# Six of 31 convolution taps per channel block as ScalarE products summed by accumulating transfers, and scans over their own input

## The chip, the cores and the metric

The kernel runs on one core of one Trainium2 chip. A core has a matrix engine (TensorE, PE in the profile; its weight loads are shown as PEld), a vector engine (VectorE, DVE), an activation engine (ScalarE, ACT), a general engine (GpSimd, POOL) and an engine that issues transfers here (SyncE, SP). Every engine takes its own instructions strictly in the order in which they were compiled, and waits on semaphores for the others. The metric is the device time of one execution in microseconds (us). A lower time is better.

## The reference

The reference is one layer of a diffusion backbone: 512 latent tokens of width 1024 with a prefix of 256 context tokens, in float32. Around the part that is changed stand two gated feed-forward blocks. The changed part is the mixer, with two branches over one input projection:

```
def conformer_branch(u_glu, lp):
    v, gt = jnp.split(u_glu, 2, axis=-1)
    u = v * jax.nn.sigmoid(gt)
    u = depthwise_conv(u, lp["w_dw"], lp["b_dw"], (15, 15))      # 31 taps, 1024 channels
    u = jax.nn.silu(layernorm(u, lp["g_ln"], lp["b_ln"]))
    return u @ lp["w_conf_out"]

def rglru_direction(xr, ...):                    # 1280 channels, forward and backward in time
    r  = sigmoid(einsum(xb, w_a) + b_a)          # blocks of 128 channels
    ig = sigmoid(einsum(xb, w_x) + b_x)
    log_a = -LRU_C * r * softplus(-lam)
    a  = exp(log_a)
    bb = sqrt(-expm1(2.0 * log_a)) * (ig * xr)
    return linear_scan(a, bb, h0, reverse)       # h[t] = a[t] * h[t-1] + bb[t]

y_lru = ((hf + hb) * gelu(proj_gate)) @ lp["w_lru_out"]
y = (sig(g_conf) * y_conf + sig(g_lru) * y_lru) @ lp["w_out"]
```

## The kernel before

Channels lie on the 128 partitions and tokens along the free dimension, so a block of 128 channels over the 512 latent tokens is one tile of 128x512, and with the context 128x768. There are eight blocks in the conformer branch and ten in the recurrent one.

Products on PE need float32 accuracy and are made from split operands. `wsplit` (L168 to 171) takes a weight tile that SP loaded (`wload`, L155 to 163, four buffers), has ACT write its rounded high half (`whi`, L152) and DVE the remainder (`wlo`, L153), three buffers each. PE then makes three products: high by high (L179), high weights by the low half of the data (L181), low weights by the high half (L183). So a weight tile goes through SP, ACT, DVE and PE in that order, and this pipeline runs through the whole kernel. The splits are issued at high priority.

The mixer is written as a list of steps (`ORDER`, L35 to 38), which a scheduler then turns into one instruction order per engine by priorities and by dependences. The steps are: `c` projects one conformer block and multiplies it by its sigmoid (`conv_block`), and `conv_taps` follows it; `f` projects one recurrent block, makes its four-tap convolution and splits it (`lru_front`); `w` loads and splits the gate weights of one block; `a` and `s` make the two gates of each direction (`lru_gates`) and then the exponent, the square root and the two scans (`lru_scan`); `g` makes two output gates (`lru_gate`); `o` multiplies the sum of the scans by its gate (`lru_out`).

`conv_taps` (L850 to 864) is the depthwise convolution of one block: ACT writes the first tap with the bias (L862), and DVE adds the other 30, each as one multiply and add over 128x512 (L864), with the result in place in `cv`. It has a priority lower by 5000 than all else, so the scheduler puts these taps into the room between other instructions. Block 7 makes five taps on PE instead and comes after the mixer, as `LATE` says.

In `lru_scan` ACT writes the decay `a` (L907), a tanh (L910) and a square root over the gate `r`; DVE multiplies into `r` (L915), then into the gated input `ig` (L916), and scans into `h`, which is `r` (L919 to 923). The sum of the two directions is written into `r` of the first one (L926). These tiles come from rotating buffers whose numbers stand in `BUFS`: three of `r`, `ig` and `a`, one pair `wgh`, `wgl` of split gate weights. When a new block takes a buffer, its first write waits until the last reader of the block before is done.

Behind the mixer stand, in this order, the merge gates of the recurrent branch (`lat_gate`, `merge_gate`, `dense`), the split of the mixer's output `y` (L153), the recurrent output projection with the gated sum (L1024), the merge gates of the conformer branch with the layer norm over all eight `cv` (L1026 to 1038) in their midst, and the conformer output projection. All of these are products on PE with new weights.

## Time and profile before

| | us |
|---|---|
| median of 3 runs | 1471.4 (1469.43 to 1475.37) |
| profiled execution, its own time | 1472.69 |
| its span in the profile | 1470.9 |
| PE busy in the span | 1423.0 (97%) |
| DVE busy | 1223.8 (83%) |
| ACT busy | 714.4 (49%) |
| POOL busy | 12.4 (1%) |

The profile is of one execution. Its span is 1.8 us shorter than the execution's own time. Busy time of PE is the time in which it had work in its pipeline. The shares are means over the whole span. The mixer fills the stretch from about 580 to 875 us, and the projections behind it start there. POOL clears the edges of two kinds of tile (`ux`, `u`) in the mixer and does little else; all transfers of the kernel before are issued by SP.

### The profile page before, as it was taken

To read this page: it belongs to the slowest core of one execution; us is meant where nothing else is said; L and a number is where in the kernel's file an instruction comes from. 1 tells how busy PE (TensorE), PEld (TensorE's weight loads), DVE (VectorE), ACT (ScalarE), POOL (GpSimd) and SP (SyncE) were. 2 spreads that over 40 slices of the span, in tenths; PEclk is the share of its full clock that TensorE was granted. 3 is DMA by queue.
4 is the path that set the end of the run, shared out by engine and by line. 5 is a ranking of instruction groups with operands and counts; after the bars stand their busy time and mean duration, and the time that the engine had idled before them with its cause. 6 is when DMAs were issued, how large, how long until landed. Compare 5 with 4: busy or idle time off the path is not lost.

```text
span 1470.9 us, 20684 instructions
## 1 busy us (share of the span) xinstructions
PE 1423.0 (97%) x8166; PEld 1283.6 (87%) x8166; DVE 1223.8 (83%) x1868; ACT 714.4 (49%) x992; POOL 12.4 (1%) x55
## 2 busy tenths in 40 slices
PE   6999999999999998999999989999999999999997
PEld 5998999989998987787788778778899989999896
DVE  6899997777878768999999999976677869678686
ACT  4632432414322446678878862236365525345253
POOL 0000000000000000000000020000000000000000
PEclk9999999999999999999999999999999999999999
DMA  9335352343543234222222223233341333323331
GB/s 375 116 129 180 115 172 72 130 143 101 186 137 137 85 100 148 82 66 78 79 73 79 72 64 93 86 116 143 103 152 49 99 103 98 112 94 99 102 100 58
DMA packets 48627, 166.41 MB, mean 113 GB/s; under 512 B 5520, under 2 KB 7824, under 8 KB 47888
## 3 DMA queue, kind: packets, MB, share of 16 engines
q1 hardware_dynamic: 48528, 165.08, 33.9%
q8 instruction: 64, 1.05, 0.3%
q14 instruction: 35, 0.29, 0.1%
HBM read 160.86 MB, written 4.19 MB: 112 GB/s over the span
## 4 chain that ended last, share of the span: by engine, by line
PE 43%; DVE 14%; issue 2%; ACT 1%; DMA 1%; DVEq 0%; ACTq 0%
PE psm L183 9%; PE psm L179 9%; PE psm L181 9%; PE psm L452 4%; PE psm L454 4%; PE psm L453 4%; DVE cv L864 3%; DVE wlo L153 2%; PE ps L179 1%; PE ps L181 1%; PE ps L183 1%; DVE ig L916 1%; DVE r L915 1%; DVE ig L900 1%; DVE r L923 1%
## 5 line engine op out<-in xcount | busy, mean ns | idle before, releaser
L152 ACT ACTIVATE whi<-raw 128x1024 fp32r<-128x1024 f32 (+2 forms) x218 | 220.3, 1012 | 333.0 <-PE psm L181 231.3
L153 DVE TENSOR_TENSOR wlo<-raw,whi 128x1024 fp32r<-128x1024 f32 (+2 forms) x218 | 252.5, 1159 | 25.7 <-ACT whi L152 25.3
L864 DVE SCALAR_TENSOR_TENSOR cv<-u,vec,cv 128x512 f32<-128x512 f32 x236 | 165.0, 741 | 0.6 <-ACT cv L862 0.3
L179 PE MATMUL psm<-H,whi 128*128 128x256 f32 (+1 forms) x496 | 151.9, 355 | 2.6 <-ACT H L152 1.7
L183 PE MATMUL psm<-H,wlo 128*128 128x256 f32 (+1 forms) x496 | 151.6, 353 | 0.3 <-DVE wlo L153 0.2
L181 PE MATMUL psm<-H,whi 128*128 128x256 f32 (+1 forms) x496 | 151.5, 353 | 0.0
L179 PE MATMUL psm<-nh,whi 128*128 128x512 f32 (+2 forms) x376 | 141.2, 383 | 4.6 <-ACT u L846 2.9
L183 PE MATMUL psm<-nh,wlo 128*128 128x512 f32 (+2 forms) x376 | 140.6, 379 | 2.4 <-DVE wlo L153 2.4
L181 PE MATMUL psm<-nl,whi 128*128 128x512 f32 (+2 forms) x366 | 138.6, 385 | 1.7 <-DVE nl L332 1.5
L179 PEld LDWEIGHTS psm<-H,whi 128*128 128x128 f32 x496 | 93.0, 189 | 16.2 <-ACT H L152 2.2
L183 PEld LDWEIGHTS psm<-H,wlo 128*128 128x128 f32 x496 | 93.6, 189 | 14.0 <-DVE wlo L153 1.3
L181 PEld LDWEIGHTS psm<-H,whi 128*128 128x128 f32 x496 | 93.9, 189 | 13.2 <-issue 0.2
L452 PE MATMUL psm<-nbx,whi 128*128 128x384 f32 x266 | 89.6, 337 | 1.3 <-ACT whi L152 0.5
L454 PE MATMUL psm<-nbx,wlo 128*128 128x384 f32 x266 | 89.4, 336 | 0.3 <-DVE wlo L153 0.3
L179 PEld LDWEIGHTS psm<-nh,whi 128*128 128x128 f32 x376 | 70.4, 189 | 18.5 <-ACT u L846 3.2
L183 PEld LDWEIGHTS psm<-nh,wlo 128*128 128x128 f32 x376 | 70.6, 189 | 16.0 <-DVE wlo L153 3.3
L181 PEld LDWEIGHTS psm<-nl,whi 128*128 128x128 f32 x366 | 68.9, 189 | 16.2 <-DVE nl L332 3.0
L642 DVE SCALAR_TENSOR_TENSOR x<-psm,m,x 128x512 f32<-128x512 f32 x64 | 47.8, 746 | 39.6 <-PE psm L183 39.6
L247 DVE SCALAR_TENSOR_TENSOR raw<-raw,cb 128x1024 f32<-128x1024 f32 x56 | 68.2, 1219 | 14.0 <-DMA raw<-in_wmod 13.8
L453 PE MATMUL psm<-nbx,whi 128*128 128x384 f32 x228 | 76.6, 336 | 0.0
L152 ACT ACTIVATE whi<-s 128x1024 fp32r<-128x1024 f32 x38 | 40.3, 1062 | 72.7 <-PE psm L181 40.0
L452 PE MATMUL psm<-nb,whi 128*128 128x256 f32 x228 | 65.8, 288 | 0.8 <-DVE t L493 0.8
(379 smaller groups left out, 3759.6 us busy)
## 6 DMA issues: line engine op xcount, KB each, us to landing
raw<-in_up SPq DMA_DIRECT2D x88, 512.0 KB, 3.7
raw<-in_wmod SPq DMA_DIRECT2D x56, 512.0 KB, 3.3
raw<-in_down SPq DMA_DIRECT2D x30, 512.0 KB, 3.9
raw<-in_down SPq DMA_DIRECT2D x24, 384.0 KB, 3.2
mod<-in_wmod SPq DMA_DIRECT2D x16, 512.0 KB, 11.1
raw<-in_wvg SPq DMA_DIRECT2D x16, 512.0 KB, 3.7
raw<-in_wout SPq DMA_DIRECT2D x11, 512.0 KB, 3.8
raw<-in_wlx SPq DMA_DIRECT2D x10, 512.0 KB, 3.7
```

What stands on the lines that cost most here:

```text
L152: S.activation(hi, src, AF.Copy)
L153: V.tensor_tensor(lo, src, f32(hi), op=ALU.subtract)
L179: T.matmul(p_, hi[:, wk, :], h, start=first, stop=False)
L181: T.matmul(p_, hi[:, wk, :], l, start=False, stop=False)
L183: T.matmul(p_, lo[:, wk, :], h, start=False, stop=last)
L247: V.scalar_tensor_tensor(o, raw, 1.0, cb[j], op0=ALU.mult, op1=ALU.mult, accum_out=out[:, j:j + 1])
L452: T.matmul(ps, hi[:, o + k, :], h, start=first and k == 0, stop=False, **kw)
L453: T.matmul(ps, hi[:, o + k, :], l, start=False, stop=False, **kw)
L454: T.matmul(ps, lo[:, o + k, :], h, start=False, stop=k == 3, **kw)
L642: V.scalar_tensor_tensor(x[:, d], ps[-1], g[:, d, 0:1], x[:, d], op0=ALU.mult, op1=ALU.add)
L864: V.scalar_tensor_tensor(o, u[:, t:t + SEQ], wdw[:, j, t:t + 1], o, op0=ALU.mult, op1=ALU.add)
L900: V.scalar_tensor_tensor(ig, ig, 1.0, xr, op0=ALU.add, op1=ALU.mult)
```

## The change

For the conformer blocks 0 to 6 the last six of the 31 taps are not made by DVE. ACT makes each as a product of the shifted input with its weight. The first one is written into a tile `o2`; the other five are written into a tile `tp`, and POOL issues a transfer for each that adds `tp` to `o2` on its way. When all are in, DVE adds `o2` to the result. `o2` and `tp` have one buffer each. The scans write over their own input `ig` instead of `r`, their sum goes straight into the tile `y`, and the output gate is multiplied in place. The gate weights get a second pair of buffers. The list of steps is the same. In the changed kernel, lines from 45 on are one number higher, and those behind `conv_taps` ten; the product is L871, the transfer L873 and the addition L874.

```diff
@@ -40,8 +40,9 @@
 UB, TC_, TA, T2 = 4, 8, 4, 8
 NPE = 8
 NB = 2
-BUFS = {"ux": 2, "acc": 1, "xr": 3, "xh": 2, "xl": 2, "r": 3, "ig": 3, "a": 3, "ge": 2, "wgh": 1, "wgl": 1}
+BUFS = {"ux": 2, "acc": 1, "xr": 3, "xh": 2, "xl": 2, "r": 3, "ig": 3, "a": 3, "ge": 2, "wgh": 2, "wgl": 2}
 PET = {7: 5}
+NDMA = {j: 6 for j in range(7)}
 SK = 3
 DGB = 3
 PAT = {6: 0, 7: 3}
@@ -860,8 +861,17 @@
         with tc.high_priority(offset=-LOW):
             if not n_pe:
                 S.activation(o, u[:, :SEQ], AF.Identity, scale=wdw[:, j, 0:1], bias=b_dw[:, j:j + 1])
-            for t in range(max(1, n_pe), TAPS):
+            n_dma = NDMA.get(j, 0)
+            for t in range(max(1, n_pe), TAPS - n_dma):
                 V.scalar_tensor_tensor(o, u[:, t:t + SEQ], wdw[:, j, t:t + 1], o, op0=ALU.mult, op1=ALU.add)
+            if n_dma:
+                o2 = Y.tile([P, SEQ], F32, name="o2", tag="o2", bufs=1)
+                for t in range(TAPS - n_dma, TAPS):
+                    tp = o2 if t == TAPS - n_dma else Y.tile([P, SEQ], F32, name="tp", tag="tp", bufs=1)
+                    S.activation(tp, u[:, t:t + SEQ], AF.Copy, scale=wdw[:, j, t:t + 1])
+                    if tp is not o2:
+                        GP.dma_start(o2, tp, accum_op=ALU.add)
+                V.tensor_tensor(o, o, o2, op=ALU.add)
 
     def lru_front(b):
         wt = wsplit(wload(io["wlx"][b // 2][:, b % 2 * 1024:b % 2 * 1024 + 1024], 1024), 0, 1024, KB)
@@ -914,7 +924,7 @@
                 last["sqrt"] = S.activation(r, r, AF.Sqrt, scale=0.25, bias=tiny)
             V.scalar_tensor_tensor(r, a, 1.0, r, op0=ALU.add, op1=ALU.mult)
             V.tensor_tensor(ig, ig, r, op=ALU.mult)
-            h = r
+            h = ig
             if d == 0:
                 V.tensor_tensor_scan(h, a, ig, 0.0, op0=ALU.mult, op1=ALU.add)
             else:
@@ -922,9 +932,8 @@
                                      op0=ALU.mult, op1=ALU.add)
                 V.tensor_tensor_scan(h[:, CTX:][:, ::-1], a[:, CTX:][:, ::-1], ig[:, CTX:][:, ::-1], h[:, 0:1],
                                      op0=ALU.mult, op1=ALU.add)
-        hsum = R[0][:, CTX:]
-        V.tensor_tensor(hsum, R[0][:, CTX:], R[1][:, CTX:], op=ALU.add)
-        return hsum
+        y[b] = blocks(Y, "y", LB + 1, F32)[0]
+        V.tensor_tensor(y[b], I[0][:, CTX:], I[1][:, CTX:], op=ALU.add)
 
     def lru_gate(i):
         raw = wload(io["wlg"][i], 2048)
@@ -942,12 +951,11 @@
             ge.append(g)
         return ge
 
-    def lru_out(b, g, hsum):
-        y[b] = blocks(Y, "y", LB + 1, F32)[0]
-        V.tensor_tensor(y[b], g, hsum, op=ALU.mult)
+    def lru_out(b, g):
+        V.tensor_tensor(y[b], y[b], g, op=ALU.mult)
 
     us = {}
-    fronts, gates, hsums, wgs, scans = {}, {}, {}, {}, {}
+    fronts, gates, wgs, scans = {}, {}, {}, {}
     for step in ORDER.split():
         kind, n = step[0], int(step[1:])
         if kind == "c":
@@ -963,13 +971,13 @@
             gs = scans.pop(n, [])
             for d in range(len(gs), 2):
                 gs.append(lru_gates(n, d, wgs[n], fronts[n]))
-            hsums[n] = lru_scan(n, gs)
+            lru_scan(n, gs)
         elif kind == "a":
             scans[n] = [lru_gates(n, 0, wgs[n], fronts[n])]
         elif kind == "g":
             gates.update(zip((2 * n, 2 * n + 1), lru_gate(n)))
         elif kind == "o":
-            lru_out(n, gates.pop(n), hsums.pop(n))
+            lru_out(n, gates.pop(n))
     regB.close()
     psum_phase("psC", 0, 8)
     regN.close()
```

On ACT in the mixer, late in it, around one block's decay (L907, L917 in the changed kernel), before:

```order
L907 ACT_TABLE_LOAD
L907 ACTIVATE a<-r,sp_4997 128x768
L152 ACTIVATE whi<-raw 128x1024
L876 ACTIVATE ux<-ps,vec 128x256
L877 ACTIVATE ux<-ps,vec 128x512
L152 ACTIVATE wgh<-raw 128x512
```

and in the changed kernel:

```order
L917 ACT_TABLE_LOAD
L917 ACTIVATE a<-r,sp_4997 128x768
L871 ACTIVATE tp<-u,vec 128x512
L920 ACTIVATE r<-r,sp_4997 128x768
L863 ACTIVATE cv<-u,vec 128x512
L871 ACTIVATE tp<-u,vec 128x512
L153 ACTIVATE whi<-raw 128x1024
L886 ACTIVATE ux<-ps,vec 128x256
```

Here `tp` is a product of the changed kernel, `whi` the high half of a weight tile and `ux` the front copy. Two products now stand between the decay and the weight split, with the tanh and a first tap moved between them.

On ACT behind the mixer, around the projection of block 7 (`sg`, `u`) and a merge gate (`t`), before:

```order
L152 ACTIVATE whi<-raw 128x1024
L846 ACTIVATE u<-psm,bh 128x512
L152 ACTIVATE whi<-raw 128x640 x2
L152 ACTIVATE whi<-raw 128x1024
L996 ACTIVATE t<-psm,bh 128x512
L152 ACTIVATE whi<-raw 128x640 x2
```

and in the changed kernel:

```order
L153 ACTIVATE whi<-raw 128x1024
L847 ACTIVATE u<-psm,bh 128x512
L871 ACTIVATE tp<-u,vec 128x512
L153 ACTIVATE whi<-raw 128x640
L871 ACTIVATE tp<-u,vec 128x512
L153 ACTIVATE whi<-raw 128x640
L871 ACTIVATE tp<-u,vec 128x512
L871 ACTIVATE o_7004<-u,vec 128x512
L153 ACTIVATE whi<-raw 128x1024
L1004 ACTIVATE t<-psm,bh 128x512
L871 ACTIVATE tp<-u,vec 128x512
L153 ACTIVATE whi<-raw 128x640
```

Products now stand between almost all weight splits, those of two convolution blocks; `o_7004` is a tile `o2`.

On DVE at the end of the mixer, around the last scans and the first sums of the layer norm (`acc`), before:

```order
L926 TENSOR_TENSOR r<-r 128x512
L864 SCALAR_TENSOR_TENSOR cv<-u,vec,cv 128x512
L153 TENSOR_TENSOR wlo<-raw,whi 128x1024
L947 TENSOR_TENSOR y_7439<-ge,r 128x512
L864 SCALAR_TENSOR_TENSOR cv<-u,vec,cv 128x512
L1029 TENSOR_TENSOR acc<-cv 128x512
L864 SCALAR_TENSOR_TENSOR cv<-u,vec,cv 128x512
L1031 TENSOR_TENSOR acc<-acc,cv 128x512
L864 SCALAR_TENSOR_TENSOR cv<-u,vec,cv 128x512
L153 TENSOR_TENSOR wlo<-raw,whi 128x1024
```

and in the changed kernel:

```order
L154 TENSOR_TENSOR wlo<-raw,whi 128x1024
L926 TENSOR_TENSOR ig<-ig,r 128x768
L874 TENSOR_TENSOR cv<-cv,o_6040 128x512
L931 SCALAR_TENSOR_TENSOR ig<-a,ig 128x256
L866 SCALAR_TENSOR_TENSOR cv<-u,vec,cv 128x512
L933 SCALAR_TENSOR_TENSOR ig<-a,ig 128x512
L866 SCALAR_TENSOR_TENSOR cv<-u,vec,cv 128x512
L936 TENSOR_TENSOR y_7521<-ig 128x512
L154 TENSOR_TENSOR wlo<-raw,whi 128x1024
L955 TENSOR_TENSOR y_7521<-y_7521,ge 128x512
L866 SCALAR_TENSOR_TENSOR cv<-u,vec,cv 128x512
L1037 TENSOR_TENSOR acc<-cv 128x512
```

`L153` and `L154` are the low halves of weights, `L864` and `L866` taps, `L926` and `L936` the sums of the two directions, `L947` and `L955` the products with the output gate, and `L874` is the new addition. The same kinds of instruction stand in both, with the addition among them and with taps and scans in other places relative to the splits.

## Rows read from the trace of the kernel before

**Rows 1.** Busy time by stretch: us, busy us (instructions) per engine, clock, DMA share, GB/s

```profile
580.00:875.00 295.00, 279.66 (x1368) 231.76 (x1367) 290.93 (x380) 234.86 (x285) 11.16 (x34) 0.99 0.22 73
875.00:985.00 110.00, 110.00 (x476) 89.04 (x475) 106.70 (x153) 28.79 (x38) 0.00 (x0) 1.00 0.32 100
```

**Rows 2.** Chain that ended last, at the mixer's end: start us, us, instruction

```profile
873.12 1.15 DVE wlo L153
874.31 0.50 PE psm L183
```

**Rows 3.** Groups of DVE, 580 to 985 us: busy us, mean ns, idle before

```profile
L864 DVE SCALAR_TENSOR_TENSOR cv<-u,vec,cv 128x512 f32<-128x512 f32 x236 | 165.0, 741 | 0.6 <-ACT cv L862 0.3
...
L915 DVE SCALAR_TENSOR_TENSOR r<-a,r 128x768 f32<-128x768 f32 x20 | 18.7, 949 | 0.0
L916 DVE TENSOR_TENSOR ig<-ig,r 128x768 f32<-128x768 f32 x20 | 18.7, 946 | 0.0
...
L926 DVE TENSOR_TENSOR r<-r 128x512 f32<-128x512 f32 x10 | 6.8, 682 | 0.0
```

**Rows 4.** Groups of ACT, 580 to 985 us

```profile
L898 ACT ACTIVATE r<-ps,bh 128x768 f32<-128x768 f32 x20 | 18.0, 900 | 19.7 <-DVE r L926 11.2 <-DVE y L947 7.4 <-PE ps L183 1.0
...
L152 ACT ACTIVATE wgh<-raw 128x512 fp32r<-128x512 f32 x10 | 6.3, 630 | 1.7 <-PE ps L181 1.5
L862 ACT ACTIVATE cv<-u,vec 128x512 f32<-128x512 f32 x7 | 5.7, 811 | 3.2 <-DVE u L847 3.0
...
L845 ACT ACTIVATE sg<-psm,bh 128x512 f32<-128x512 f32 x7 | 4.8, 679 | 0.0
```

**Rows 5.** Transfers: count, KB, us to landing; with L160, issue ns, and landings

```profile
raw<-in_wvg SPq DMA_DIRECT2D x12, 512.0 KB, 3.7
raw<-in_wga SPq DMA_DIRECT2D x9, 256.0 KB, 2.6
mod<-in_wmod SPq DMA_DIRECT2D x16, 512.0 KB, 11.1
L160 SPq DMA_DIRECT2D raw<-in_wga x9: 327/328/328, 586.8 to 803.9; - x9
DMA to landing us min/median/max: 2.5/3.6/5.1
```

**Rows 6.** Groups of POOL, whole span: one of the zeroings in the mixer

```profile
L872 POOL MEMSET ux<- 128x2 f32 x10 | 1.0, 100 | 243.4 <-DVE xr L884 155.1 <-PE psm L183 88.3
```

**Rows 7.** ACT by time, three places: start us, us, instruction, [idle before, releaser]

```profile
596.34 0.91 ACT L331 ACTIVATE nhc<-t,m 128x256 fp32r<-128x256 f32 x2 [3.38 <-DVE t L330]
...
723.27 1.03 ACT L907 ACTIVATE a<-r,sp 128x768 f32<-128x768 f32 x1
...
725.86 1.04 ACT L152 ACTIVATE whi<-raw 128x1024 fp32r<-128x1024 f32 x1
...
817.64 1.03 ACT L907 ACTIVATE a<-r,sp 128x768 f32<-128x768 f32 x1
818.58 1.04 ACT L152 ACTIVATE whi<-raw 128x1024 fp32r<-128x1024 f32 x1
```

**Rows 8.** DVE by time, the low halves that follow two of these

```profile
727.86 1.22 DVE L153 TENSOR_TENSOR wlo<-raw,whi 128x1024 fp32r<-128x1024 f32 x1
...
819.83 1.21 DVE L153 TENSOR_TENSOR wlo<-raw,whi 128x1024 fp32r<-128x1024 f32 x1
```

**Rows 9.** ACT by time behind the mixer: four weight splits

```profile
884.86 1.06 ACT L152 ACTIVATE whi<-raw 128x1024 fp32r<-128x1024 f32 x1 [4.12 <-PE psm L181]
...
888.26 0.74 ACT L152 ACTIVATE whi<-raw 128x640 fp32r<-128x640 f32 x1 [1.76 <-PE psm L181]
...
897.10 1.06 ACT L152 ACTIVATE whi<-raw 128x1024 fp32r<-128x1024 f32 x1 [4.70 <-PE psm L181]
...
928.38 0.74 ACT L152 ACTIVATE whi<-raw 128x640 fp32r<-128x640 f32 x1 [2.66 <-PE psm L181]
```

**Rows 10.** PE by time: first product with the split of 888.26

```profile
897.13 0.39 PE L179 MATMUL psm<-yh,whi 128*128 128x512 f32 x1
```

## The prediction

> **What bounds the kernel now.** I read the busy times by stretch first, then the chain that ended last, then what each engine waits for. From 580 to 875 us, the mixer, VectorE (DVE) is busy 290.9 of 295.0 us, the matrix engine (PE) 279.7 and ScalarE (ACT) 234.9. From 875 to 985 PE is busy all 110.0 us and ACT only 28.8 [rows 1]. So the mixer is bound by DVE with PE close behind, and what follows it by PE. The chain says the same: it runs through DVE up to a weight split that ends at 874.3 us, and hands over to PE there [rows 2]. What is taken from DVE counts only if it stood ahead of that split; later taps lie beside a busy PE. The most that the mixer can give back is PE's idle time in it, 295.0 - 279.7 = 15.3 us. The second thing to see is how ACT and DVE hang together: both take their work strictly in order, ACT makes the high halves of the weights, DVE the low halves from them, PE needs both.
>
> **The change part by part.**
>
> DVE. Removed are 42 taps (seven blocks, six each) of 741 ns, 31.1 us; added are seven additions, one per block, which are like the 682 ns tensor-tensor sum of the same size [rows 3]: 4.8 us. That is 26.3 us less in all, but the order decides where. Counted over DVE's whole order from the first weight split of the mixer to the one that hands over, 129 taps stand ahead of it before and 128 now, with four of the new additions. The scheduler has moved other blocks' taps into the room. Four splits of the mixer's output, three sums of the layer norm and one multiplication with the gate, eight instructions of 0.68 us, now stand behind it. So the stretch that bounds gets 0.7 - 2.7 + 5.5 = 3.5 us shorter on DVE. The other 23 us leave the stretch where PE is always busy, and I price them at nothing; PE is their cover, and if it waited for a conv block there, up to those 23 us would return.
>
> In-place scans. A multiplication that writes over its own input takes 946 ns, one of the same size that also reads another tile 949 ns [rows 3], so I price the scans' new target at nothing on DVE; both bounds are within 0.1 us per block. What it changes is when buffers come free: r is released after the multiplication and not after the sum or the gate product. ACT waits 11.2 + 7.4 = 18.6 us for these two in the mixer [rows 4]. DVE is busy during these waits, so they are no path today; I price them at nothing (bounds: 0 and a gain of 18.6 us). The second pair of gate weight buffers is the same case: ACT is idle 1.7 us ahead of filling the one pair [rows 4], and I leave that at nothing too.
>
> ACT products. 42 activations of 128x512 with a per-partition factor; the nearest row takes 0.68 us [rows 4], together 28.6 us, of which some 26 products stand in the mixer, where ACT is idle 60.1 us. Their own time has room. What does not is the wait between two of them. There is one tp tile, so each product waits until the transfer of the one before has landed, and ACT's whole queue (weight splits, gate activations, front copies) stands behind it. Call D the time from the end of a product until its sum has landed. Before shows no transfer issued by POOL and none that adds, so D is bounded by neighbours: a plain 256 KB load lands in 2.6 us, a 512 KB one in 3.7, the slowest load of this stretch in 5.1, and loads queued behind others in 11.1 [rows 5]. An adding transfer takes in the product and the old sum, 2 x 256 KB, so I take 3.7, and 0.33 for the issue (SP's step, same rows): D = 4.0 us.
>
> POOL. Its queue is in order as well: the zeroings of ux and u wait for DVE, 155.1 us in all for ux [rows 6], and several adding transfers now stand behind such a zeroing. At their places ACT comes to the next product no earlier than DVE releases the zeroing, so I add nothing; if it did, ACT would stand for the difference.
>
> Mixer, three places where the product that waits is ahead of something that is used at once.
> First, at 593 us: ACT is idle 3.38 us until 596.34 [rows 7] and then makes the context operand nhc, which PE waits for. Now a first product, a product, its transfer, another product and a split stand ahead: 592.96 + 0.68 + 0.68 + 4.0 + 0.68 + 1.05 = 600.0, 3.7 us late. DVE has three more taps ahead of its next split there, 2.2 us of work pulled forward: 1.5 us lost.
> Second, at 725 us: product, tanh, an activation of 0.81 us [rows 4] that stood earlier before, product. The transfer lands at 724.3 + 0.7 + 4.0 = 729.0, the product ends at 729.7, and the split that started at 725.86 is 3.8 us late. DVE took it 0.96 us after its end [rows 7, 8]: 2.9 us lost.
> Third, at 818 us: the same pattern ahead of the split of 818.58, which starts at 818.67 + 0.68 + 4.0 + 0.68 = 824.0, 5.4 us late; DVE stood 0.21 us behind it [rows 7, 8]: 5.2 us lost.
> The sum is 9.6 us; the largest alone is 5.2, for a stall is paid in full only where DVE has caught up again with ACT. I take 7.5.
>
> Behind the mixer. Between the split at 884.86 and the one at 928.38 us ACT's order now holds 12 products that wait for a transfer. They form one chain: 12 x (4.0 + 0.68) = 56.2 us, where PE's pace gives 928.38 - 884.86 = 43.5 [rows 9]. Short by 12.7. The lead that weight splits have eats part of it: the split of 888.26 ends at 889.00 and PE first uses it at 897.13 [rows 9, 10], less some 0.8 us for DVE's low half, about 7 us. But ACT also comes to this stretch late: three chained products with an addition between follow the last square root, some 11 us of waiting and work, and I put the lateness at 4 us (bounds 0 and 11). So PE loses 12.7 + 4 - 7 = 9.7 us here, and it has no idle time from which to win it back. The chain costs nothing if 12 x (D + 0.68) stays under 43.5 us, that is D under 2.9.
>
> Here a rule of the Trainium skill speaks, in DMA: Bandwidth & Descriptors, section Anatomy of one DMA — SWDGE (gpsimd) path: a transfer issued by GpSimd takes about 2.0 us and its bytes at 436 GB/s, which for 256 KB is an estimate of 2.6 us. By that rule D would stay under the point named above, and the no-change rival below would hold. No row of before shows such a transfer.
>
> Sum: -3.5 + 7.5 + 9.7 = +13.7 us. The profiled execution took 1472.7 us, span 1470.9 and 1.8 around it; 1472.7 + 13.7 = 1486.4. It stood 1.3 us above the median of 1471.4, which gives 1485.
>
> **The rivals.**
> Faster. The freed r tiles let ACT run ahead, its 60 us of idle time in the mixer take products and waits, and PE gets back half of its 15.3 us of idle time: 1471.4 - 8 = 1463. For it: 18.6 us of ACT's waits are for the very tiles that are released earlier. Against it: DVE follows ACT by 0.2 to 1 us at the places above, so ACT is not ahead where it matters. It decides as soon as D is below about 2.5 us. Chance 0.17.
> No change. D = 2.9, the 256 KB row and the issue: the chain behind the mixer fits, each of the three places loses 1.1 us less (9.6 - 3.3 = 6.3, and 4.9 in the same proportion that I took), DVE's 3.5 us pay for most of it: +1.4, 1473. Chance 0.16.
> Much slower. POOL gets to issue its transfers only in the gaps between DVE's instructions, and waits for some four of them, 4 x 0.74 = 3 us [rows 3]: D = 7. The chain is 12 x 7.68 = 92.2 us, 48.7 over; + 4 - 7 = 45.7 lost; the three places cost 9 more; -3.5 + 16.5 + 45.7 = +58.7, 1530. For it: DVE is busy 106.7 of the 110.0 us [rows 1]. Against it: POOL's zeroings take 100 ns each beside the same busy DVE [rows 6], so it doesn't stand behind DVE with everything. Chance 0.15. The Trainium skill has such a rule in SBUF — State Buffer, section SBUF: two separate sides: GpSimd cannot write a transfer's descriptors while DVE holds the port that the two share, and a transfer of about 620 ns then took about 3100; with two inputs in SBUF, as here, DVE takes that port only against a GpSimd operation that reads SBUF. The row on the zeroings agrees with the exception; no row of before shows a transfer.
> Forecast, D from 3.3 to 5.1: at 5.1 the chain is 69.4 us, +22.9 after the lead, the places +10, in all +29; at 3.3 the chain is 47.8 us, +1.3, the places +5.8, in all +4. So 1475 to 1501 around 1485. Chance 0.52.
>
> **How the numbers follow.** What a measurement of this kernel can tell from no change is 0.5%, 7.4 us. Faster: 0.17. The lower end of the forecast is within that, about 0.05, so same is 0.16 + 0.05 = 0.21 and slower 0.47 + 0.15 = 0.62. The range from 1463 to 1520 leaves out about 0.08 below, half of the faster case, and 0.11 above, most of the much slower one; it holds cases of both signs, and the forecast alone stands between 1475 and 1501.
>
> **What would show it.** Transfers from POOL of about 4 us from product to landing; ACT waiting for a DMA ahead of L871, some 100 us in all; DVE idle for ACT near 600, 725 and 820 us; PE idle between 890 and 940 for high halves of the weights; about 970 us the last taps gone from DVE without PE being earlier. I am wrong if D is under 2.9 us, if PE stays at full use from 875 to 985, or if the mixer ends earlier than 875.

## The result, and the profile after

The changed kernel takes 1499.6 us (median of 5 runs, 1495.4 to 1502.3) against 1472.5 before (5 runs): a ratio of 1.0184, 95% interval 1.017 to 1.0198, 27 us slower. The direction and the mechanism were forecast; the size was twice the forecast (+13.7 us). The profiled execution took 1502.3 us, with a span of 1500.4. It is the slowest of the five, so a difference read from the traces (29.5 us between the spans) comes out some 2 us larger than one between the medians (27.1).

Busy times of the two stretches that were read before [rows 1], in the same columns:

```profile
580.00:875.00 295.00, 277.91 (x1344) 231.03 (x1343) 282.10 (x365) 236.50 (x287) 19.69 (x58) 0.97 0.33 90
875.00:985.00 110.00, 92.75 (x366) 72.00 (x365) 82.01 (x115) 41.45 (x65) 26.67 (x17) 0.91 0.45 108
```

Behind the mixer PE was busy all 110.0 us and made 476 products; now it is idle for 17.3 us, its mean granted clock is 0.91, and it makes 366. The stretch is not merely longer: the engine that had no idle time there has some.

The mixer moved less. The starts of the same weight tiles' low halves on DVE (in the traces) show where the time goes:

| low half | before, us | after, us | later by |
|---|---|---|---|
| at the mixer's start | 585.58 | 583.62 | -1.9 |
| behind the first place | 607.22 | 611.91 | +4.7 |
| handover to PE [rows 2] | 873.05 | 877.95 | +4.9 |
| last ahead of block 7's last diagonals | 932.32 | 956.82 | +24.5 |
| well behind | 995.01 (high half) | 1023.94 | +28.9 |

So the mixer lost 4.9 + 1.9 = 6.8 us, and the stretch behind it 28.9 - 4.9 = 24.0. The 1.9 us by which the mixer starts earlier are not the change's. Up to there PE, DVE and ACT execute the same instructions in the same order in every kernel of this document, and yet the low half at the mixer's start comes between 3.4 us earlier (e16) and 3.6 us later (e8, e2) than before. A difference of a few us between two traces is read with that spread in mind.

The groups that answer to [rows 3, 4, 5, 6], from the lines, DMA and POOL views of the kernel after (ACT's from 580 to 985 us, POOL's over the span):

```profile
L871 ACT ACTIVATE tp<-u,vec 128x512 f32<-128x512 f32 x35 | 25.2, 720 | 74.9 <-DMA o<-tp 74.9
...
L908 ACT ACTIVATE r<-ps,bh 128x768 f32<-128x768 f32 x20 | 18.0, 898 | 0.0
```

```profile
L873 POOL DMA_DIRECT2D o<-tp x35: 859/859/1002, 592.6 to 956.5; - x35
...
DMA to landing us min/median/max: 3.2/3.3/5.7
```

```profile
L873 POOL DMA_DIRECT2D o<-tp x35 | 30.4, 868 | 262.0 <-ACT tp L871 214.6 <-ACT o L871 37.1 <-DVE acc L891 5.6
L990 POOL TENSOR_SCALAR_AFFINE_SELECT ident<-ident 128x128 f32<-128x128 f32 x1 | 13.5, 13467 | 0.1
```

ACT stands 74.9 us ahead of products for a transfer that has to land (some 100 were forecast), and no longer waits for r (19.7 us before; 5.8 us are left ahead of the other gate, `ig`). A transfer occupies POOL for 0.86 us and lands 3.3 us after its issue.

The chain behind the mixer, ACT by time (three links, and the end; a link is a product, its transfer and the wait of the next product for the landing):

```profile
895.57 0.71 ACT L871 ACTIVATE tp<-u,vec 128x512 f32<-128x512 f32 x1
...
946.25 0.72 ACT L871 ACTIVATE tp<-u,vec 128x512 f32<-128x512 f32 x1 [3.76 <-DMA o<-tp]
...
950.70 0.72 ACT L871 ACTIVATE tp<-u,vec 128x512 f32<-128x512 f32 x1 [2.22 <-DMA o<-tp]
...
955.44 0.72 ACT L871 ACTIVATE tp<-u,vec 128x512 f32<-128x512 f32 x1 [3.39 <-DMA o<-tp]
956.07 0.72 ACT L153 ACTIVATE whi<-raw 128x640 fp32r<-128x640 f32 x1
956.70 0.68 ACT L858 ACTIVATE dg<-ident,vec 128x128 f32<-128x128 f32 x2
```

Twelve links take 955.44 - 895.57 = 59.9 us, 4.99 each; the shortest takes 4.44, so D is 3.72 at best and 4.27 on average (4.0 was taken). At the end stands what had been overlooked: two of the five diagonals `dg` for block 7's taps on PE (a diagonal is the 128x128 matrix of a tap's weights with which PE makes that tap). PE by time shows who waits:

```profile
931.57 0.50 PE L180 MATMUL psm<-nh,whi 128*128 128x512 f32 x1 [3.90 <-ACT whi L153]
...
945.92 2.74 PE L859 MATMUL psm<-u,dg 128*128 128x512 f32 x6
957.13 3.78 PE L859 MATMUL psm<-u,dg 128*128 128x512 f32 x4 [8.48 <-ACT dg L858]
```

Half of PE's idle time is the one wait of 8.48 us for these diagonals. In the kernel before ACT wrote them when PE let go of their buffer, with hardly any lead: ACT had stood 0.35 us for the first, and PE loaded it at 930.56 (weight loads by time), 0.69 us after it was written (ACT by time, before):

```profile
929.47 0.40 ACT L857 ACTIVATE dg<-ident,vec 128x128 f32<-128x128 f32 x1 [0.35 <-PE psm L858]
930.33 0.40 ACT L857 ACTIVATE dg<-ident,vec 128x128 f32<-128x128 f32 x1 [0.46 <-PE psm L858]
```

PE's clock falls with its idle time. Busy times in stretches of 10 us, after (the number behind the busy times is the granted clock, as in [rows 1]):

```profile
920.00:930.00 10.00, 7.67 (x34) 6.01 (x32) 6.45 (x9) 2.23 (x4) 1.72 (x2) 1.00 0.52 127
...
950.00:960.00 10.00, 2.87 (x5) 1.32 (x5) 2.25 (x3) 3.28 (x6) 1.72 (x2) 0.62 0.62 130
960.00:970.00 10.00, 10.00 (x39) 7.83 (x38) 8.77 (x12) 2.01 (x3) 0.00 (x0) 0.87 0.10 27
970.00:980.00 10.00, 10.00 (x45) 8.27 (x45) 9.75 (x15) 2.23 (x3) 0.00 (x0) 1.00 0.37 118
```

The clock has two levels, 1.2 and 2.4 GHz, and these are means of the two. Around the long wait it is 0.62, and still 0.87 in the next stretch, where PE is busy throughout and makes 39 products and not 45. Behind the two next longest waits it fell too: to 0.77 from 900 to 910 us (a wait of 3.51 us) and to 0.83 from 930 to 940 (3.90). Over 875 to 985 us an estimate of what this makes PE's products longer is (1 - 0.91) x 92.75 = 8 us, beside the 17.3 of idle time; the forecast had not priced it. But not all of it is lost time. Up to the diagonals ACT's chain waits for transfers, and once for DVE, never for PE, so that a faster PE would only have stood longer for them. What the clock adds to the delay stands behind the diagonals: PE's first product with them starts 26.1 us later than before (957.13; 930.99, the seventh of the ten in its row, before), the next weight splits come 28.9 us later, and PE waits for nothing in between. That is 2.8 us.

### The profile page after: what moved, and what is told of

Its sections match the earlier page's. It is cut to its first block, busy times and chain, and to the rows that moved or that the text cites. A ratio compares the mean times of both kernels' runs of the same rounds, so it can differ in the third digit from the quotient of the medians.

```text
span 1500.4 us, 20796 instructions
## 1 busy us (share of the span) xinstructions
PE 1433.7 (96%) x8166; PEld 1289.9 (86%) x8166; DVE 1204.8 (80%) x1833; ACT 738.4 (49%) x1034; POOL 47.3 (3%) x90
## 4 chain that ended last, share of the span: by engine, by line
PE 39%; DVE 12%; DMA 5%; ACT 2%; issue 2%; POOL 1%; DVEq 0%; ACTq 0%
PE psm L180 8%; PE psm L182 8%; PE psm L184 8%; PE psm L453 4%; DMA o<-tp 4%; PE psm L455 4%; PE psm L454 4%; DVE cv L866 3%; DVE wlo L154 2%; PE ps L180 1%; PE ps L182 1%; PE ps L184 1%; DVE ig L926 1%; POOL ident L990 1%; DVE ig L929 1%
## 5 line engine op out<-in xcount | busy, mean ns | idle before, releaser
L153 ACT ACTIVATE whi<-raw 128x1024 fp32r<-128x1024 f32 (+2 forms) x218 | 219.9, 1010 | 273.5 <-PE psm L182 183.0
L154 DVE TENSOR_TENSOR wlo<-raw,whi 128x1024 fp32r<-128x1024 f32 (+2 forms) x218 | 252.6, 1159 | 64.1 <-ACT whi L153 63.4
L866 DVE SCALAR_TENSOR_TENSOR cv<-u,vec,cv 128x512 f32<-128x512 f32 x194 | 139.4, 744 | 1.7 <-ACT cv L863 0.3
L180 PEld LDWEIGHTS psm<-nh,whi 128*128 128x128 f32 x376 | 71.5, 192 | 18.6 <-ACT whi L153 4.3
L153 ACT ACTIVATE whi<-s 128x1024 fp32r<-128x1024 f32 x38 | 40.3, 1062 | 71.6 <-PE psm L182 38.8
## 6 DMA issues: line engine op xcount, KB each, us to landing
mod<-in_wmod SPq DMA_DIRECT2D x16, 512.0 KB, 11.2
```

Source lines behind the costliest of these rows:

```text
L153: S.activation(hi, src, AF.Copy)
L154: V.tensor_tensor(lo, src, f32(hi), op=ALU.subtract)
L180: T.matmul(p_, hi[:, wk, :], h, start=first, stop=False)
L866: V.scalar_tensor_tensor(o, u[:, t:t + SEQ], wdw[:, j, t:t + 1], o, op0=ALU.mult, op1=ALU.add)
```

## The experiments

The theory: ACT's in-order queue stands behind the one product buffer, and the chain of links behind the mixer sets the end. Rivals: the transfers disturb the weight loads or DVE; the scans share the blame; the products' own time on ACT is too much. All kernels below are edits of the changed one unless they say otherwise. "Later by" compares profiled executions at the weight split that starts at 995.01 us before; one trace of each kernel was kept.

**The parts alone (e1, e2).** e1 has `NDMA = {}`; e2 is the kernel before with `NDMA` and the new end of `conv_taps`.

> The in-place scans and the second pair of gate weight buffers alone; all taps are on VectorE as before. Theory (the loss is ScalarE's queue standing behind the single product buffer): no products, so no loss: 1472 us, within 4. Rival (the scans' new buffer lifetimes reorder the mixer, and the products are not to blame): 1485 or more. Faster rival: ScalarE's 18.6 us of waits for r go and VectorE gains: 1464.

> The products and transfers alone, with the scans and buffers of before. Theory: the whole loss stands, 1499 us within 5, with ScalarE waiting about 75 us ahead of the products for the transfers. Rival (scans share the blame): 1480 to 1490.

Measured: 1471.4 us, ratio 0.9982 (0.997 to 0.9995), for e1, and 1486.6, ratio 1.008 (1.0055 to 1.0105), for e2. The scans and the pair of buffers are harmless by themselves. But the products alone cost 13 us, not 27. That misses the theory's number and lies in the rival's range (1480 to 1490), though e1 leaves the scans no blame of their own. This stayed open until e13 and e14.

**More buffers (e3).**

```diff
-BUFS = {... "wgh": 2, "wgl": 2}
+BUFS = {... "wgh": 1, "wgl": 1}
-o2 = Y.tile(..., tag="o2", bufs=1)
+o2 = Y.tile(..., tag="o2", bufs=2)
-... Y.tile([P, SEQ], F32, name="tp", tag="tp", bufs=1)
+... Y.tile([P, SEQ], F32, name="tp", tag="tp", bufs=5)
```

> The changed kernel with five buffers of the product tile and two of the sum tile (one pair of gate weight buffers, to make room). The same 35 transfers move the same bytes and still follow one another. Theory: ScalarE no longer waits for a transfer inside a block, so the stretch behind the mixer is bound by TensorE again: 1474 us, between 1468 and 1480, ScalarE's wait for transfers under 15 us. Rival (the transfers take the weight loads' bandwidth, or GpSimd's issue disturbs VectorE): as slow as the changed kernel, 1495 or more.

Measured: 1479.9 us, ratio 1.0038 (1.0026 to 1.005). The window 880 to 990 us of this kernel, and its products on ACT:

```profile
880.00:990.00 110.00, 110.00 (x476) 89.05 (x475) 85.45 (x117) 32.61 (x47) 4.36 (x5) 1.00 0.41 112
```

```profile
L871 ACT ACTIVATE tp<-u,vec 128x512 f32<-128x512 f32 x35 | 22.8, 713 | 5.7 <-DMA o<-tp 5.7
```

PE is busy all 110 us again, at full clock, with the same 35 transfers of the same bytes. So not the transfers but waiting for them costs the time behind the mixer; the rival of bandwidth falls. The order of ACT's products changes with the buffers too, so this run alone does not prove it. What is left, 6 us, is lost in the mixer: its first low half is 1.3 us early, the one at the handover 5.0 us late, and nothing more is lost up to the split of 995.01. ACT waits only 5.7 us for transfers there, all near 608 to 616 us; what else the 6 us are is not shown.

**No transfers (e4).** All six products write the sum tile.

```diff
-tp = o2 if t == TAPS - n_dma else Y.tile([P, SEQ], F32, name="tp", tag="tp", bufs=1)
+tp = o2
-if tp is not o2:
-    GP.dma_start(o2, tp, accum_op=ALU.add)
```

> The six products of a block all write the sum tile one over the other, and no transfer is made; this leaves out five of the six products' sums. ScalarE's work and VectorE's are those of the changed kernel. Theory: 1469 us (3.5 us less on VectorE ahead of the handover), at most 1473. Rival (ScalarE's 25 us of products themselves delay the weight splits): 1480 or more.

Measured: 1474.6 us, ratio 1.0004 (0.9992 to 1.0016). ACT's own time for 42 products fits, and taking 42 taps off DVE wins nothing even when the sum is free. The expected gain of 3.5 us was not there.

**The identity matrix (e5).** In the kernel after, POOL by time shows a second thing that was overlooked:

```profile
880.03 0.86 POOL L873 DMA_DIRECT2D o<-tp  x1 [3.72 <-ACT tp L871]
880.57 0.54 POOL L989 MEMSET ident<- 128x128 f32 x1
881.18 13.47 POOL L990 TENSOR_SCALAR_AFFINE_SELECT ident<-ident 128x128 f32<-128x128 f32 x1
```

The matrix from which the diagonals are made stood ready at 855.6 us before; now it stands in POOL's queue behind a transfer that waits for ACT. e5 makes it at the kernel's start:

```diff
-    ident = C.tile([P, P], F32, name="ident")      # behind the mixer
+    ident = const.tile([P, P], F32, name="ident")  # behind tiny, at the start
```

> The changed kernel with the identity matrix of block 7's products on TensorE made at the start of the kernel and not behind the products' transfers in GpSimd's queue (it took 13.47 us there, until 894.65 us, and ScalarE waited 4.38 us for it). Theory (the chain of products behind the mixer sets the end): it starts 4.4 us earlier and ends as much earlier: 1495, between 1492 and 1497. Rival (the late identity matrix is the loss itself): 13 us or more come back, 1486 or less. Rival (it lies beside the chain): no change, 1499.

Measured: 1499.0 us, ratio 1.0177 (1.016 to 1.0194). The chain did start 4.0 us earlier (891.54) and took the same 60.1 us, and the split at 995.01 was 25.1 us late in place of 28.9; but the timed runs show no more than 1 us, and the intervals overlap. It isn't the loss itself, and whether it is worth the 4 us that the trace shows stays open, the more so as the changed kernel's trace is of its slowest execution.

**No products for blocks 5 and 6 (e6).**

```diff
-NDMA = {j: 6 for j in range(7)}
+NDMA = {j: 6 for j in range(5)}
```

> Products and transfers for blocks 0 to 4 only; ScalarE's order in the mixer stays word for word that of the changed kernel, and behind the identity matrix 3 waiting products stand in place of 12. Theory (the chain is the loss behind the mixer): 1472.5 + 7 lost in the mixer + 1 to 4 for the late identity matrix, 1480 to 1484, and TensorE busy for at least 107 of the 110 us from 880 to 990. Rival (transfers and scans slow the mixer itself, or the weight loads): 1490 or more.

Measured: 1483.2 us, ratio 1.007 (1.0055 to 1.0085); from 875 to 985 us PE is busy 108.8 us at a clock of 1.00. With ACT's order unchanged up to the chain's third product, taking ten of the twelve waiting products from behind the mixer (two are left, and not three) gives back 17 us; in its trace 2.3 us are lost behind the mixer and not 24.0. This is the cleanest evidence for the chain. It is not the chain alone: at the same place in POOL's order the identity matrix took 1.25 us here and not 13.47, and by e5's trace that is worth some 4 us (24.0 - 19.8, in the table below).

**What the adding costs (e7).** `accum_op=ALU.add` is left out.

> The same transfers from the same queue in the same order, but plain copies that do not add, which leaves out the sums of the products. Theory: the adding costs something of the landing time, 3.3 to some 2.9 us, the chain of 12 gets 12 x 0.4 = 5 us shorter: 1494, between 1490 and 1498. Rival (adding is free, the time is GpSimd's issue and the landing as such): 1499. Rival (adding is what makes it slow): landing 2.0 us or less, 1483 or less.

Measured: 1479.8 us, ratio 1.0045 (1.0027 to 1.0062). Its transfers:

```profile
L873 POOL DMA_DIRECT2D o<-tp x35: 538/538/672, 596.0 to 940.2; - x35
...
DMA to landing us min/median/max: 2.2/2.4/5.2
```

A plain copy lands in 2.4 us and not 3.3, and is issued in 0.54 and not 0.86. The chain of the same 12 links takes 939.23 - 890.58 = 48.7 us, 4.05 each. 11 us less of chain came with 20 us less of time (18.8 between the traces, at the split of 995.01). The order on ACT, DVE, POOL and PE is that of the changed kernel through the whole chain, so no other order explains the rest. The chain also started 5.0 us earlier, and PE loses 0.1 us behind the diagonals and not 2.8: its clock is 1.00 from 880 to 990 us, with PE busy 106.3 of 110.0. 11.2 + 5.0 + 2.7 = 18.9. But part of the earlier start isn't the copy's own. POOL by time:

```profile
880.44 1.31 POOL L990 TENSOR_SCALAR_AFFINE_SELECT ident<-ident 128x128 f32<-128x128 f32 x1
```

The identity matrix, at the same place in the same order, was ready at 881.75 us and not at 894.65, and ACT didn't wait for it. The theory had the sign but a quarter of the size; the time is the one of the last rival (1483 or less), the landing is not (2.0 or less). So the adding makes the chain 11 us longer, and with it brings the long wait that lowers the clock; the identity matrix's share is not the adding's as far as is shown. At the D of this kernel, 4.05 - 0.73 = 3.3, the forecast had +4 us in all; 0.45% are 6.6.

Here the Trainium skill, DMA: Bandwidth & Descriptors, section Anatomy of one DMA — SWDGE (gpsimd) path, can be set beside a measurement: its 2.0 us and 436 GB/s give an estimate of 2.6 us for 256 KB, and the plain copy took 2.4 to landing. For the adding transfer, 3.3 and 0.86 for the issue, the section has no figure.

**Sums on GpSimd (e8).** `GP.tensor_tensor(o2, o2, tp, op=ALU.add)` in place of the transfer, with three buffers of tp.

> The sums are made by GpSimd's own additions in place of the transfers, with three buffers of the product tile. Theory from the identity matrix's row (a GpSimd operation that reads SBUF ends 0.15 us after some instruction of VectorE's and waits while these follow one another without a gap): each addition takes 3 to 14 us where VectorE is busy, ScalarE waits for them, 1500 or more. Rival (GpSimd adds beside VectorE at its own pace, about 1 us each): 1476 or less.

Measured: 1511.4 us (one run). The additions and the taps beside them:

```profile
L873 POOL TENSOR_TENSOR o<-o,tp 128x512 f32<-128x512 f32 x35 | 60.8, 1737 | 216.5 <-ACT tp L871 131.6 <-ACT o L871 83.0
```

```profile
L866 DVE SCALAR_TENSOR_TENSOR cv<-u,vec,cv 128x512 f32<-128x512 f32 x182 | 149.0, 847 | 5.1 <-ACT cv L860 3.6 <-ACT cv L863 0.3
```

Each addition took 1.7 us (1.3 to 2.7), less than the theory's 3 to 14, and ACT waited only 17.9 us for them. But DVE's taps went from 744 to 847 ns beside them. Both answers missed the mechanism: the price is paid by DVE, which bounds the mixer. Between the low halves at the mixer's start and at the handover DVE is busy 312.3 us (366 instructions), against 283.6 (367) in e4, which has nearly the same instructions on DVE; this stretch got 30.0 us longer than before.

**All diagonals ahead of the chain (e9).**

```diff
-PET = {7: 5}
-DGB = 3
+PET = {7: 4}
+DGB = 4
```

> The changed kernel, with block 7's taps on TensorE made from four diagonal matrices that ScalarE writes together ahead of the chain of products (four buffers in place of three, four taps on TensorE in place of five, one more tap on VectorE). In the changed kernel ScalarE writes two of five diagonals behind the last product of the chain and TensorE, which takes its work in order, stands 17.8 us for them. Theory (the lead of the weight splits doesn't help because these two diagonals have none): TensorE's wait moves to the last splits, which have some 7 us of lead: 7 + 1 us come back, 1492, between 1489 and 1494. Rival (ScalarE's chain alone sets the pace, whatever stands at its end): only the 1 us of the tap less, 1498.

The 17.8 us of this expectation count the waits of the weight load and of the product together; PE's own wait was the 8.48 us shown above. Measured: 1499.9 us, ratio 1.0167 (1.0138 to 1.0197), four runs from 1492.5 to 1500.5. PE's waits from 880 to 990 us:

```profile
PE psm L184 <- DVE wlo L154: 4.0, 2, 3.7
PE psm L182 <- DVE y L154: 3.7, 1, 3.7
PE psm L180 <- ACT whi L153: 3.6, 1, 3.6
```

The wait for diagonals is gone and another has come in its place, of 3.7 us. DVE by time shows what is late next:

```profile
962.39 0.69 DVE L874 TENSOR_TENSOR cv<-cv,o 128x512 f32<-128x512 f32 x1 [2.54 <-DMA o<-tp]
963.12 0.69 DVE L1039 TENSOR_TENSOR acc<-acc,cv 128x512 f32<-128x512 f32 x1
963.73 5.47 DVE L866 SCALAR_TENSOR_TENSOR cv<-u,vec,cv 128x512 f32<-128x512 f32 x7
969.11 0.82 DVE L154 TENSOR_TENSOR wlo<-raw,whi 128x640 fp32r<-128x640 f32 x1
```

The addition of the last block waits for the last transfer, and seven taps stand between it and the low half that PE needs. The forecast's lead of 7 us does not show in the timed runs: expected 1492, measured 1500. In the trace part of it does. The last product comes 76.5 us behind the handover, in the changed kernel 77.5, and 18.3 us are lost behind the mixer and not 24.0: beyond the earlier end 4.7 us came back (the clock's share in them is not taken apart). Its mixer started 3.7 us later than that of the changed kernel's trace, for no reason in the code, which hides most of this in the profiled time (1499.9 against 1502.3). The two ratios, 1.0167 and 1.0184, leave room for 7 us less as well as for 2 more. That the diagonals were PE's wait is shown; that they kept the lead from helping is backed by one trace and not confirmed by the times.

**The small edits (e10, e11).** e10 is e1 with one pair of gate weight buffers; e11 is the kernel before with two.

> The in-place scans alone, with one pair of gate weight buffers as in the kernel before. Theory: the earlier release of r is what gave 2.7 us with the scans and buffers alone, so 1470.5 to 1472. Rival (the second pair of buffers gave it): 1473.5 to 1475.

> The second pair of gate weight buffers alone, in the kernel before. Theory: nothing, 1473.5 within 1.5 (ScalarE waits 1.7 us for it in all). Rival (it gave the 2.7 us): 1471 or less.

Measured: 1473.8, ratio 0.9998 (0.9986 to 1.001), and 1469.8, ratio 0.9981 (0.9968 to 0.9994). By the times the expectation is reversed: the scans over their own input are worth nothing, the second pair of buffers is worth 3 us (0.9 to 4.7 by its interval). For the scans this isn't clean. In e10's trace the mixer is 4.8 us shorter than before, and 5.3 us are lost behind it, where the identity matrix took longest of all and ACT stood 6.38 us for it (POOL and ACT by time):

```profile
869.27 16.20 POOL L990 TENSOR_SCALAR_AFFINE_SELECT ident<-ident 128x128 f32<-128x128 f32 x1
```

```profile
885.51 0.99 ACT L858 ACTIVATE dg<-ident,vec 128x128 f32<-128x128 f32 x3 [6.38 <-POOL ident L990]
```

What the scans are worth without that wait is not shown.

**Fewer products (e12, e15, e16).** `NDMA = {j: 3 ...}`. e12 has four buffers of tp, two of o2 and one gate pair; e15 two, one and two pairs; e16 is e15 with the scans of before.

> Three taps of a block in place of six as products (two transfers per block, 14 in all), four buffers of the product tile and two of the sum tile, one pair of gate weight buffers. Theory: half of what five buffers still lost in the mixer (6.4 us) goes and nothing is lost behind it: 1476, between 1473 and 1479. Faster rival (a small share on ScalarE fits its idle time): 1470 or less.

> Three products per block, two buffers of the product tile, the in-place scans and the second pair of gate weight buffers; 2 products in the chain. Theory: three products per block were worth nothing either way (1472.7), the pair wins 3: 1470, between 1468 and 1472. Rival (the products take what the pair wins): 1473 or more.

> The same with the scans of before. Theory: the same time within 1.5 us, since the scans alone were worth nothing. Rival (the scans' earlier release of r is what makes room for the products): 1473 or more while the version with in-place scans is at 1470.

Measured: 1472.7, ratio 0.9996 (0.9983 to 1.0008); 1478.6, ratio 1.0045 (1.0027 to 1.0063); 1475.9, ratio 1.0023 (1.0009 to 1.0037). ACT waited 0, 22.6 and 14.9 us for transfers. e12 came out below its theory (1473 to 1479) by a little and e15 above its own (1468 to 1472), where its rival had it; e16 is 2.7 us from e15 and not 1.5, with intervals that overlap. Where ACT doesn't wait, products cost nothing and win nothing (e12, e4); what the pair wins is lost with two buffers of tp and one of o2. e11 and e1, which have the pair and no products, stay the fastest kernels, by 0.2%.

**Why the parts don't add up (e13, e14).** e13 is e2 with the second pair; e14 is the changed kernel with one pair.

> The products with the second pair of gate weight buffers, with the scans of before. Between block 7's two writes of diagonals stand 10 products that go through the transfer, 9 with the products alone, 13 in the changed kernel. Theory (time follows the number of links in the chain, 5 us each): 1486.6 + 5 - 3 (what the pair wins) = 1488.5, between 1486 and 1491. Rival (the parts simply add): 1483.5. Rival (the pair is what turns bad with the products): 1495 or more.

> The products with the in-place scans, with one pair of gate weight buffers. 11 products stand between block 7's two writes of diagonals. Theory (number of links): 1486.6 + 2 x 5 = 1496, between 1493 and 1499. Rival (the parts simply add): 1486.5. Rival (the scans are what turns bad with the products): as the changed kernel, 1499.5.

Measured: 1487.9, ratio 1.0114 (1.0095 to 1.0133), and 1486.8, ratio 1.01 (1.0085 to 1.0116). e13 is near the count's number, e14 misses it by 9 us and is where addition puts it. So the number of links alone doesn't set the time. ACT's rows of e14:

```profile
888.68 0.73 ACT L871 ACTIVATE tp<-u,vec 128x512 f32<-128x512 f32 x1
...
940.52 0.72 ACT L871 ACTIVATE tp<-u,vec 128x512 f32<-128x512 f32 x1 [3.75 <-DMA o<-tp]
...
943.91 0.68 ACT L858 ACTIVATE dg<-ident,vec 128x128 f32<-128x128 f32 x2
```

| kernel | first to last product of the chain, us | links | last diagonals behind the handover by | PE's wait for them | lost behind the mixer |
|---|---|---|---|---|---|
| before | | | 56.4 | | |
| after | 895.57 to 955.44 | 12 | 78.8 | 8.48 | 24.0 |
| e5 | 891.54 to 951.68 | 12 | 74.5 | 6.53 | 19.8 |
| e14 | 888.68 to 940.52 | 10 | 62.3 | 2.61 | 4.9 |
| e7 | 890.58 to 939.23 | 12 | 62.0 | 2.75 | 4.6 |
| e13 | 887.31 to 940.18 | 9 | 64.6 | none | 8.3 |
| e2 | 895.13 to 939.88 | 8 | 60.3 | none | 4.0 |
| e9 | 899.02 to 957.63 | 12 | ahead of the chain | none | 18.3 |

The handover is each kernel's own low half that starts at 873.05 us before, so the spread ahead of the mixer and what the mixer lost are left out. PE's waits at the diagonals, PE by time in e5, e14 and e7:

```profile
953.37 2.93 PE L863 MATMUL psm<-u,dg 128*128 128x512 f32 x3 [6.53 <-ACT dg L862]
```

```profile
944.36 1.99 PE L859 MATMUL psm<-u,dg 128*128 128x512 f32 x4 [2.61 <-ACT dg L858]
```

```profile
940.92 1.99 PE L859 MATMUL psm<-u,dg 128*128 128x512 f32 x4 [2.75 <-ACT dg L858]
```

In the four kernels where PE stands for the diagonals, the loss is their delay against before, less the 1.0 us between ACT and PE there, plus what the clock costs behind them (2.8 us in the changed kernel, 2.7 in e5, 0.1 in e14 and e7): 24.2, 19.8, 5.0 and 4.7 us, against 24.0, 19.8, 4.9 and 4.6. So the end of the chain does set the time behind the mixer in these four. In e2 and e13 PE doesn't wait for the diagonals; its waits of up to 0.93 and 3.23 us are for halves of weights along the chain. What they lost is smaller and this account does not cover it. The chain ends at 940 with 8, 9 or 10 links, since each begins elsewhere and some links also wait for DVE to release the sum tile (4.1 us at one in e13). Against e14 the changed kernel has two links more (8.0 us), and its chain starts 10.6 us later behind the handover (17.6 against 7.0), 4.4 of them by the identity matrix (13.2 in e5; it took 13.47 us against 0.99 in e14): 18.6 us, against 19.2 more that are lost behind the mixer. Neither small edit is bad with the products by itself; what all three together make of the scheduler's order, and of the identity matrix, is.

## Why the prediction was wrong

**Right.** What bounds the kernel; that taps behind the handover are worth nothing (e4); that ACT's in-order queue with one tp tile is the cost and not ACT's time (e3, e4); D (4.27 on average for 4.0); that POOL's issue is not held up by DVE (859 ns at least and at the median, 1002 at most, with DVE busy 282.1 of 295.0 us). On this the Trainium skill's exception in SBUF — State Buffer, section SBUF: two separate sides, agrees with the trace: DVE's operations with two inputs did not keep GpSimd from writing descriptors. It agrees on the other side too: the identity matrix, a GpSimd operation that reads SBUF, took from 0.29 us (e5, at the kernel's start) to 16.20 us (e10) for the same 128x128.

**The step that failed** is the term behind the mixer, +9.7 us, which measured 24.0. The mechanism was right and the sum too small, in four parts, against the rows:
- The lead. "The lead that weight splits have eats part of it ... about 7 us." It ate next to nothing. The chain ends at two diagonals, which before had 0.35 + 0.69 = 1.0 us between ACT and PE (an estimate from the rows above, counted in the rest); the lead was read at a split in the middle. 7.0 us.
- The links: 4.99 us and not 4.68, 12 x 0.31 = 3.7 us.
- The lateness of ACT at the chain's start. The split of 884.86 came 11.3 us late (13.2 from the mixer's start), PE's handover 6.8: 6.4 us and not 4, in part the identity matrix, an operation in POOL's queue behind a transfer that the section on POOL had not looked for. 2.4 us.
- The rest, 1.2 us: PE's clock costs 2.8 us behind the diagonals, from which their 1.0 us goes and 0.5 because ACT wrote them sooner behind the last split (0.63 us and not 1.09); 1.3 in these rounded terms.

7.0 + 3.7 + 2.4 + 1.2 = 14.3 = 24.0 - 9.7. The runs back the chain and its links (e6, e7, and the table above). For the lead, the largest part, there are traces alone: in e9's 4.7 us of it came back, in its times nothing that can be told from the spread. PE did stand between 890 and 940 us, as forecast, 3.51 us for a low half and 3.90 for a high one; the longest wait was not among the signs that had been named.

**The mixer** lost 6.8 us where -3.5 + 7.5 = 4.0 was forecast. The total was near by luck: the parts were wrong one by one. The first place cost 6.6 us (4.7 + 1.9 in the table) and not 1.5: its first transfer took 5.7 us to land and PE stood 5.93 us for nhc. The second cost 1.2 us of its 2.9: its split, at 732.86, is 7.0 us late where the one ahead of it was 5.8. The third cost nothing of its 5.2: its split, at 827.26, is 8.7 us late where the one ahead of it was 9.7. A fourth, not counted, at 755 us, cost 2.4 (8.9 to 11.3): there ACT waited 4.97 us for a transfer ahead of a split. And DVE gave back 6.1 us between the low halves of 843.45 (11.0 us late) and 877.95 (4.9) and not 3.5. These parts come to 4.1 us and not to 6.8; the others are small steps both ways between them. (Times of the kernel after.)

**The rivals.** "Much slower" held that POOL waits for DVE with its issues; the issue rows exclude it. "No change" put the edge at D = 2.9; e7, at 3.3, still lost 6.6 us, and no run has a D below the edge. "Faster" needed room on ACT that is used; e4 and e12 had it and won nothing.

## What to carry to other kernels

A queue's slack is to be read at the instructions that stand behind the last waiting one, and not only at a typical one: here the chain ended at an operand that PE had loaded 0.7 us after it was made, and the lead of 7 us read in the middle wasn't there (one trace, e9, shows some of it back when that operand is moved). Work that is moved to an idle engine is cheap only if it waits for nothing there; with one buffer and a transfer of 4 us per link, 25 us of work became 75 us of waiting, ahead of everything that the engine makes for others. A long stall costs more than its wait: behind waits of 8.48 and 6.53 us PE's low clock cost another 2.8 and 2.7 us, behind 2.75 and 2.61 only 0.1. Ahead of a wait that another engine ended, the low clock cost nothing here. And one operation of a queue can move a whole chain: the same identity matrix took 13.47 us in the changed kernel and 1.31 in e7, in the same order.

## What the hardware showed

- A 256 KB SBUF-to-SBUF transfer from GpSimd that adds lands in 3.3 us (median of 35) and takes GpSimd 0.86 us; without adding it is 2.4 and 0.54 (e7).
- GpSimd's affine select of 128x128 took 0.29 to 16.20 us. In 15 of the 18 traces (0.48 to 16.20 us) it ended 0.15 to 0.16 us after the end of one of DVE's instructions, which followed each other almost without a gap meanwhile; in e15, where it fell into a gap of DVE's, it took 0.29. Which of DVE's instructions it ends behind is not shown: in the changed kernel, e6 and e7, with the same order up to there, it took 13.47, 1.25 and 1.31.
- An addition of 128x512 on GpSimd takes 1.7 us beside a busy DVE, and DVE's taps get 14% longer (e8).
- A second buffer pair for a 0.63 us split, for which ACT had waited 1.7 us in all, was worth 3 us (e11; 0.9 to 4.7 by the interval).
